# A hybrid decoder block on eight cores: list-scheduled engine queues, attention beside the gate matmuls, and an MLP in token blocks with all its weights resident

## Chip, cores, metric

One Trainium2 chip, all 8 cores, one launch. Each core computes 2048 tokens by itself; no core talks to another. The metric is device time of the slowest core in microseconds (us). Most executions agree within 0.3% (16 of the 20 runs of the kernel before lie between 920.6 and 924.6 us). In some, one die (cores 0 to 3 or 4 to 7) shows a lower granted clock and the time is longer. Such executions are called slow and stay out of all comparisons.

## The reference, cut

```python
# x: (2, 8192, 1024) float32; 8 query heads and 2 KV heads of 64; window 128; D_FF 4096
u = rms_norm(h, norm_mix)
z = u @ w_in                      # pooled groups 512 | q 512 | k 128 | v 128 | two gates of 1024
y_pool = pool_mixer(z[..., :512]) @ p_pool        # trailing means over 2, 4, 8, 16 tokens
y_attn = swa_sink_attention(q, k, v, sinks) @ p_attn   # window 128, ALiBi, one sink per head
h = h + (sigmoid(gate_pool) * y_pool + sigmoid(gate_attn) * y_attn) @ w_out
a = relu(rms_norm(h, norm_mlp) @ w_up)
h = h + (a * a) @ w_down
return rms_norm(h, norm_final)
```

## The kernel before

Bfloat16 matmuls with float32 sums. A recorder (`P.op`) notes what each operation reads and writes, derives semaphore waits, and emits each engine's instructions in the order in which the program names them. The stages follow each other over all 2048 tokens. Cut to what the argument touches:

```python
# weights, issued by GpSimd, float32 -> bf16 on the way; columns cut out of wide matrices
for g in range(4):
    dma("pool", WS[0][:, :, g*128:(g+1)*128], w_in_v[:, :, g*128:(g+1)*128], "ws0_%d" % g)
# ... and five more of this kind; x tiles are issued by SyncE:
for t in range(19):
    if t < 17:
        dma("sp", xs, src, "xs%d" % (t % 3))
        act(SQJ, xs, AF.Square, scale=1.0 / 32.0, accum=st_ss[t % 4])
    # ... power on GpSimd, scale on VectorE, transposes, then projection jobs

for i in range(19):               # attention: all 16 blocks, nothing else beside them
    if i < 16:
        att_s(i); att_exp(i)                              # scores, Exp
    if 0 <= i - 1 < 16:
        att_decay(i - 1); att_pv(i - 1); att_norm(i - 1)  # products, values, 1/sum
    if 0 <= i - 2 < 16:
        att_ot(i - 2)
# ... gates for all tokens (4 pairs of column blocks), output projection, then:
seq = [(sg, s) for sg in range(4) for s in range(4)]      # MLP: a quarter of D_FF at a time
for i in range(len(seq) + 1):
    if 1 <= i < len(seq):
        mlp_up(*seq[i])
    if i >= 1:
        mlp_down(*seq[i - 1])     # adds its part to h in SBUF: 4 evictions per output half
```

The softmax here doesn't subtract the row's maximum and nothing guards it: scores larger than these inputs give would overflow.

## Time and profile before

| | before |
|---|---|
| time, median of 20 runs beside the changed kernel | 922.3 us |
| span of the profiled run | 919.3 us |
| TensorE busy | 812.2 us (88%) |
| GpSimd busy | 219.4 us (24%) |

The prediction shows the lines behind this.

(In all lines shown, `arena` is the one SBUF tensor in which every tile of the kernel lies, so operations are told apart by engine and shape.)

### The profile page before, as it was taken

What the parts mean: (1) busy time and instruction counts of PE and PEld (TensorE: products, weight loads), DVE (VectorE), ACT (ScalarE), POOL (GpSimd) and SP (SyncE); (2) the same over time, 40 slices, a digit from 0 to 9 for tenths busy, and PEclk for the clock granted to TensorE, in tenths of its full rate; (3) what the DMA queues carried; (4) which work ended last, traced back from release to release, by engine and by line L of the source; (5) the groups of instructions that cost most, each with busy time, mean ns of one, the idle gap of its engine ahead of it and who ended that gap; (6) DMA issues with size and microseconds to landing.
All of it is one profiled execution on the core that took longest, in us unless ns stands there. A gap on an engine that the chain in (4) does not pass through costs nothing.

```text
span 919.3 us, 12450 instructions; the slowest of 8 cores (915.9 to 919.3 us)
## 1 busy us (share of the span) xinstructions
PE 812.2 (88%) x4121; PEld 377.2 (41%) x4121; DVE 359.1 (39%) x550; ACT 271.3 (30%) x439; POOL 219.4 (24%) x204
## 2 busy tenths in 40 slices
PE   1489964556999999999999999999999999999993
PEld 1344422233444444444444444444444444444441
DVE  2372166875222222256523222333223333224545
ACT  2253546543222222245531222111222111223322
POOL 3021724221232322221131111211121111113432
PEclk9999985555999999999999999999999999999997
DMA  9760009400023410199229000830009100001213
GB/s 181 157 184 2 1 8 142 80 1 1 1 23 47 52 18 1 39 222 248 43 43 163 2 1 1 123 61 1 0 1 156 28 1 1 1 1 70 91 70 137
DMA packets 37230, 55.20 MB, mean 60 GB/s; under 512 B 6960, under 2 KB 21552, under 8 KB 37168
## 3 DMA queue, kind: packets, MB, share of 16 engines
q0 software_dynamic: 28816, 27.95, 22.1%
q1 hardware_dynamic: 8352, 26.46, 8.9%
q8 instruction: 34, 0.56, 0.2%
q14 instruction: 28, 0.23, 0.1%
HBM read 73.97 MB, written 8.39 MB: 90 GB/s over the span
## 4 chain that ended last, share of the span: by engine, by line
PE 76%; DVE 11%; issue 4%; DMA 4%; ACT 3%; POOL 1%; DVEq 0%; POOLq 0%; ACTq 0%; SPq 0%
PE psum L377 74%; DVE arena L392 9%; ACT arena L388 3%; DMA arena<-w_in 3%; PE psum L381 2%; DMA arena<-x 1%; DVE arena L397 1%; POOL arena L392 1%; DVE arena L402 0%; POOL arena L412 0%; DVE arena L645 0%; DVEq L191 0%; POOLq L277 0%; ACTq L191 0%; ACT arena L407 0%
## 5 line engine op out<-in xcount | busy, mean ns | idle before, releaser
L377 PE MATMUL psum<-arena 128*128 128x512 bf16 (+2 forms) x3776 | 788.7, 374 | 67.1 <-DVE arena L392 44.4
L377 PEld LDWEIGHTS psum<-arena 128*128 128x128 bf16 x3776 | 355.3, 100 | 487.6 <-issue 95.7
L392 POOL TENSOR_TENSOR arena<-arena 128x512 bf16<-128x512 f32 (+3 forms) x167 | 191.4, 1146 | 655.1 <-ACT arena L388 339.7
L388 ACT ACTIVATE arena<-psum 128x512 f32<-128x512 f32 (+1 forms) x224 | 145.4, 658 | 439.0 <-PE psum L377 431.2
L392 DVE TENSOR_TENSOR arena<-psum,arena 128x512 f32<-128x512 f32 (+2 forms) x225 | 144.8, 654 | 164.4 <-PE psum L377 130.8
L392 DVE TENSOR_TENSOR arena<-arena 128x512 bf16<-128x512 f32 (+4 forms) x125 | 102.0, 838 | 164.0 <-ACT arena L388 161.1
L388 ACT ACTIVATE arena<-arena 128x1024 bf16<-128x1024 f32 (+1 forms) x82 | 74.3, 929 | 104.5 <-DVE arena L392 49.9
L402 DVE SCALAR_TENSOR_TENSOR arena<-arena,psum 128x512 f32<-128x512 f32 x64 | 43.8, 688 | 125.7 <-PE psum L377 122.6
L381 PE MATMUL psum<-arena 128*128 128x128 bf16 x345 | 33.2, 245 | 26.9 <-DVE arena L422 10.4
L402 DVE SCALAR_TENSOR_TENSOR arena<-arena 128x1024 f32<-128x1024 f32 (+1 forms) x20 | 29.7, 1486 | 39.7 <-POOL arena L392 23.9
L381 PEld LDWEIGHTS psum<-arena 128*128 128x128 bf16 x345 | 24.5, 110 | 41.0 <-issue 40.6
L407 ACT COPY arena<-psum 128x512 bf16<-128x512 bf16 (+3 forms) x41 | 21.9, 552 | 57.2 <-PE psum L381 36.6
L397 DVE TENSOR_SCALAR arena<-arena 128x1 f32<-128x1 f32 x66 | 19.3, 305 | 38.2 <-ACT arena L388 37.1
L402 DVE SCALAR_TENSOR_TENSOR arena<-psum,arena 128x512 f32<-128x512 f32 x32 | 22.1, 692 | 22.2 <-PE psum L377 22.2
L407 ACT CAST arena<-psum 128x512 bf16<-128x512 f32 (+1 forms) x26 | 14.6, 560 | 29.0 <-PE psum L377 28.8
L412 POOL DMA_DIRECT2D arena<-w_in x14 | 12.6, 912 | 16.5 <-DVE arena L392 15.9
L388 ACT ACTIVATE arena<-psum,arena 128x512 bf16<-128x512 f32 x16 | 11.1, 781 | 5.9 <-PE psum L377 5.9
L388 ACT ACTIVATION_READ_ACCUMULATOR arena<-arena 128x1 f32 x49 | 9.1, 186 | 0.0
L412 POOL DMA_DIRECT2D arena<-w_down x4 | 3.5, 878 | 22.5 <-PE psum L377 22.5
L645 DVE RECIPROCAL arena<-arena 128x8 f32<-128x8 f32 x16 | 3.3, 203 | 1.7
L412 POOL DMA_DIRECT2D arena<-w_up x4 | 3.8, 940 | 0.0
L412 POOL DMA_DIRECT2D arena<-p_pool x4 | 3.1, 780 | 0.0
(11 smaller groups left out, 7.5 us busy)
## 6 DMA issues: line engine op xcount, KB each, us to landing
arena<-x SPq DMA_DIRECT2D x32, 512.0 KB, 7.6
arena<-w_up POOLq DMA_DIRECT2D x4, 2048.0 KB, 18.7
arena<-w_down POOLq DMA_DIRECT2D x4, 2048.0 KB, 24.0
y<-arena SPq DMA_DIRECT2D x16, 512.0 KB, 2.6
arena<-w_in POOLq DMA_DIRECT2D x9, 512.0 KB, 11.6
arena<-w_out POOLq DMA_DIRECT2D x1, 2048.0 KB, 32.1
arena<-w_in POOLq DMA_DIRECT2D x4, 256.0 KB, 16.2
arena<-w_in POOLq DMA_DIRECT2D x1, 1024.0 KB, 30.3
```

What stands on the lines that cost most here:

```text
L377: P.op("pe", lambda e: e.matmul(out, lhsT, rhs, start=start, stop=stop), r=[lhsT, rhs], w=[out])
L381: P.op("pe", lambda e: e.transpose(out, in_, IDENT), r=[in_, IDENT], w=[out])
L388: return e.activation(out, in_, func, bias=bias, scale=scale, **kw)
L392: P.op(eng, lambda e: e.tensor_tensor(out, in0, in1, op), r=[in0, in1], w=[out])
L397: return e.tensor_scalar(out, in0, s1, None, op0)
L402: P.op(eng, lambda e: e.scalar_tensor_tensor(out, in0, scalar, in1, op0, op1), r=[in0, in1] + ([scalar] if isap(scalar) else []), w=[out])
L407: P.op("act", lambda e: e.copy(out, in_), r=[in_], w=[out])
L412: P.op(q, lambda e: e.dma_start(out=out, in_=in_), r=[in_], w=[out], dma_slot=slot)
L645: P.op("dve", lambda e: e.reciprocal(rd, den), r=[den], w=[rd])
```

## The change

Its intent: take attention, pooling and the output projection off the path by laying them between dense matmuls. A list scheduler replaces program order: every operation has a modelled cost, and each engine takes the operation that can start first among the next few in its program. Attention of block s + 1 and the output projection of block s - 1 lie in the gates of block s (512 tokens). The MLP takes one block at a time with all of `w_up` and `w_down` resident, and sums over all of D_FF in PSUM. The weights are re-laid on the host into contiguous rows. Cut to the core:

```diff
+WINDOW = {"pe": 24, "act": 24, "dve": 24, "pool": 12, "sp": 8}
+DMA_FIXED = 2.0
+DMA_RATE = 300e3
+    def schedule(self):            # ... dependency graph; then, until nothing is left:
+            for e in self.ENGINES:
+                for n in queue[e][:WINDOW[e]]:
+                    # ... t = when engine and inputs are free; keep the earliest
+            if ops[0].dma_slot is not None:
+                bus = max(bus, end) + ops[0].dma_bytes / DMA_RATE   # one bus for all DMA
+                end = bus + DMA_FIXED
-    w_in_d = din("w_in", [D, 3328])
+    wp_d = din("wp", [128, 10, 1024])   # contiguous: 2 or 4 tiles of 4 KB in one run
+    wg_d = din("wg", [8, 128, 3072])    # gate and mixer weights of one column block: 12 KB
+    wu_d = din("wu", [8, 128, 4096])    # 16 KB
+    wd_d = din("wd", [8, 128, 4096])
+    for s in range(4):
+        e = e_units(s)                             # gates of block s
+        f = f_units(s - 1) if s else []            # output projection of block s - 1
+        # ... extra: att_units of block s + 1, second norm, loads of w_up and w_down
+        run(dense, extra)
+    for s in range(4):
+        if s:
+            for fc in range(32):
+                up_unit(s, fc)
+        for ti in range(4):
+            for hh in range(2):
+                down_half(4 * s + ti, hh)          # 32 matmuls into one bank, one eviction
```

## The prediction

> **What bounds the kernel now.** I read the page from the top: busy shares, the clock row of the 40 slices, then busy time by stage (stage limits taken from the TensorE timeline), then the timeline inside the worst stage. The page:
>
> ```profile
> PE 812.2 (88%) x4121; PEld 377.2 (41%) x4121; DVE 359.1 (39%) x550; ACT 271.3 (30%) x439; POOL 219.4 (24%) x204
> ...
> PEclk9999985555999999999999999999999999999997
> ```
>
> TensorE is the only engine near its limit, and the clock row shows four slices (23 us each) at half clock. Busy time, clock and DMA in six stretches; columns are length, then busy us (instructions) of PE, PEld, DVE, ACT, POOL, then granted clock, DMA share, GB/s:
>
> ```profile
> 0.00:134.00 134.00, 91.79 (x533) 47.00 (x533) 53.56 (x70) 55.27 (x98) 39.16 (x35) 1.00 0.42 90
> 134.00:223.00 89.00, 45.84 (x389) 23.86 (x390) 64.70 (x129) 46.59 (x68) 28.70 (x25) 0.50 0.46 60
> 223.00:393.00 170.00, 170.00 (x783) 76.74 (x782) 44.53 (x65) 38.80 (x65) 47.80 (x41) 0.99 0.18 27
> 393.00:460.00 67.00, 60.88 (x356) 28.93 (x355) 39.51 (x60) 34.34 (x45) 9.36 (x17) 1.00 0.75 171
> 460.00:902.00 442.00, 439.76 (x2048) 199.51 (x2048) 147.34 (x216) 93.11 (x157) 89.91 (x84) 1.00 0.23 43
> 902.00:919.00 17.00, 3.61 (x16) 1.50 (x16) 9.09 (x13) 3.45 (x6) 4.73 (x3) 0.69 0.39 155
> ```
>
> The stretches are: first norm with projections, attention, gates, output projection, MLP, tail. Gates and MLP are solid matmul: 170.0/783 = 217.1 ns and 442/2048 = 215.8 ns for one of 512 columns. These are my unit costs. From the TensorE timeline of the first stage, eight 128-column transposes and the matmuls after them:
>
> ```profile
> 46.76 0.61 PE L381 MATMUL psum<-arena 128*128 128x128 bf16 x8 [0.29 <-DVE arena L397]
> 47.20 1.89 PE L377 MATMUL psum<-arena 128*128 128x512 bf16 x8
> ```
>
> The next instruction starts 0.44 us after the first of eight: 55 ns each. For the 65-column matmuls the trace has only half-clock groups (15 in 1.14 us, the last taking 0.21: 66 ns); 50 ns at full clock is my estimate.
>
> The program has 3472 matmuls of 512 columns (64 of them scores), 393 of 128, 256 of 65: 2048 x 0.2158 + 1424 x 0.2171 + 393 x 0.055 + 256 x 0.050 = 442.0 + 309.2 + 21.6 + 12.8 = 785.6 us. The span is 919.3, so 133.7 us are lost. By stage, length less its own work: first 134 - 84 = 50; attention 89 - 30 = 59; gates 0; output projection 67 - 59 = 8; MLP and tail 459.3 - 442 = 17. Inside attention one 128-token block takes 5 us, and TensorE waits for VectorE twice in each:
>
> ```profile
> 160.64 0.60 PE L377 MATMUL psum<-arena 128*128 128x65 bf16 x8 [1.22 <-DVE arena L392]
> 162.35 0.54 PE L377 MATMUL psum<-arena 128*128 128x65 bf16 x7 [1.10 <-DVE arena L392]
> 162.70 0.62 PE L381 MATMUL psum<-arena 128*128 128x128 bf16 x4
> 163.25 1.20 PE L377 MATMUL psum<-arena 64*128 64x512 bf16 x5
> 165.67 1.14 PE L377 MATMUL psum<-arena 128*128 128x65 bf16 x15 [1.22 <-DVE arena L392]
> ```
>
> [...] 0.50 throughout attention although these waits are only 1.1 to 1.2 us. [...] 1.00 for 442 us of dense MLP on all eight cores. [...] the 512-column product on VectorE, in attention beside GpSimd's and in the MLP window 483 to 600:
>
> ```profile
> L392 DVE TENSOR_TENSOR arena<-arena 128x512 bf16<-128x512 f32 x48 | 46.6, 1025 | 8.9 <-ACT arena L388 8.9
> ```
> ```profile
> L392 DVE TENSOR_TENSOR arena<-arena 128x512 bf16<-128x512 f32 x18 | 12.5, 692 | 46.2 <-ACT arena L388 46.2
> ```
>
> [...] So loads issued from SP and from GpSimd share the bandwidth, while the new scheduler books them one after another on a single 300 GB/s bus. [...] the share is my assumption.
>
> **The change, part by part.** Arithmetic barely moves. V comes out as 136 matmuls of 128 columns in place of 32 of 512, 8 of 128 and 17 transposes; the halo of the pooled groups shrinks to 32 of 16 columns. Now 3440 x 512, 472 x 128, 256 x 65, 32 x 16: 442.0 + 302.2 + 26.0 + 12.8 + 1.8 = 785 us. The gain has to come from the 134 us.
>
> Attention's block now lies between gate and projection matmuls. The order of the changed program has, in the gates, second scores, four or five groups of dense matmuls (4.3 to 4.8 us), then the value matmuls. What must fit there: Exp 1.02, two products of 0.69, a y product or two of 0.69, hops: 3.5 to 4.5 us. It fits, just. VectorE per 512 tokens of the middle stage: 16 x 0.69 gates + 8 x 0.69 mixes + 16 x 0.69 decays + 4 x 1.1 value norms + 11 output projection and second norm = 43 us beside 65 us of matmuls. GpSimd keeps only powers and pooling adds, so 0.69 holds. Of 59 us I leave 6 here.
>
> The start. Tiles 0 to 4 of x and the first constants are 2.9 MB, and 2.1 MB or more of weights share the bandwidth. In the output-projection stage, DMA share 1.0, 245 GB/s landed; with weights counted as the float32 read, about 325. At half of that, tile 4 lands near 3.5 + 18 = 21.7 us; square 1.25, power 0.55, scale 0.75, transposes, eviction 1.23 and hops make 5: first dense projection at 26.5 us, with 5 us of work done before. Lost: **21.5**, plus **1.7** for the cold clock.
>
> Then the order shows a fault. Because the scheduler's bus puts x tiles 6 on behind all weights, their squares stand in ScalarE's queue behind the last eviction of block 0, and the block-0 projections (20 us of matmuls) have nothing behind them. From the end of block 0 (46.5): five squares at 1.25 and two Exp pieces, then eviction of tile 8: about 56. TensorE has 1.8 us of work in these 9.3: **7.5** lost, **2** for the re-cooled clock, **2.5** for evictions queued behind late tiles in block 1.
>
> The MLP's start. The second fault in the order: three w_down pieces of 2.1 MB can load only when the output projection ends, and the last w_up piece is queued behind them. Two transfers of that kind issued together took this long in the kernel now (last column, us to landing):
>
> ```profile
> arena<-w_up POOLq DMA_DIRECT2D x4, 2048.0 KB, 18.7
> arena<-w_down POOLq DMA_DIRECT2D x4, 2048.0 KB, 24.0
> ```
>
> (2048 KB landed as bf16 is 4.2 MB read), so 8.4 MB take about 25 us and the piece lands 26 us after the projection ends. TensorE has ten groups of 1.73 and a transpose set, 17.8 us: **8** lost, **2** more for the clock.
>
> MLP: accumulating over all of K removes 96 of 128 evictions, but they lay beside matmuls, so nothing is gained but a calmer end. The tail after the last matmul is one tile: add 0.8, square 1.35, scalars and power 0.95, scale 1.4, store 3: **7.6**, in place of 17.3.
>
> Sum: 785 + 21.5 + 1.7 + 7.5 + 2 + 2.5 + 6 + 10 + 7.6 = 844 us span. The profiled time was 2.5 above the span, so **846 us**, 8% less.
>
> **The rivals.** *A: the order fits badly.* Queues are fixed in advance from modelled times. Where a tile is late, everything behind it on that engine waits, also what is ready. For: the two faults above. Against: three PSUM banks and 24-deep reordering leave slack. It would put 25 to 35 us more into the first 130: 870 to 880. *B: everything hides.* x is favoured at the DMA, the tiles come by 20 us, the waits before the MLP are covered: 785 + 15 + 3 + 8 + 2.5, some 815. Against: the static order keeps the handover gap even if data is early. *C: VectorE becomes the bound of the middle stage,* if products stay at 1025 ns: 16 x 0.33 adds 5 to 43 of 65 us. Still below, but with in-order queues it could cost 10 to 15 us: 860. [...]
>
> **Range and chances.** Uncertain are the start (plus or minus 8), the handover (0 to 12), the middle (3 to 20), the MLP's start (0 to 14). Added as independent they give about 17 to either side, and A and C lean up: 824 to 872. Faster by over 2% needs under 903, far outside A: 0.97. Within 2% 0.02, slower 0.01 [...].
>
> **What would show it.** TensorE busy share near 93%, clock row at full from the third slice on except near 50 us and one dip at the MLP's start; first run of 512-column matmuls at 24 to 29 us; a gap of 7 to 10 us near 47 to 56 us put down to VectorE; no wait of TensorE over 1.5 us in the gates; one wait of 5 to 11 us on a w_up transfer; the product group near 0.70 us; GpSimd busy below 100 us; end 7 to 9 us after the last matmul. Wrong it would be if the granted clock drops in the MLP, if middle-stage waits sum to over 20 us, or if projections are still waiting for x tiles after 70 us.

## More of the kernel before

One more view matters later and was not weighed enough: the DMA queues (queue, packets, MB landed, share of the 16 engines' time). q0 is GpSimd's queue, q1 SyncE's; weights land as bf16, half of what is read (the page's 73.97 MB read from HBM are 2 x 27.95 + 26.46 - 8.39 MB written).

```profile
q0 software_dynamic: 28816, 27.95, 21.9%
q1 hardware_dynamic: 8352, 26.46, 8.7%
```

A weight packet here is on average 27.95 MB / 28816 = 1 KB landed, 2 KB read.

## The result

| | before | after |
|---|---|---|
| time, median | 922.3 us (20 runs) | 876.4 us (10 runs) |
| ratio, 95% interval | | 0.9502 [0.9493, 0.9511] |
| TensorE busy | 88% | 91% |
| GpSimd busy | 219.4 us | 74.9 us |

A ratio is the mean time of one kernel's fast runs over that of the other's in the same rounds, so not quite the ratio of the medians. The change gains 5.0%, not 8.2%; 876 lies 4 us above the predicted range. The page of the changed kernel (40 slices of 21.9 us):

```profile
PE   0295999999999999699984999999999999999996
...
PEclk9996999999999999899996999999999999999999
DMA  8973314600212169989384212000220002200021
```

TensorE is weak only in slices 1, 2 and 4 and in two dips, slice 17 and slices 21 and 22. The DMA digit is 7 to 9 in the first three slices and where each dip begins; only slice 4 waits with little DMA under way. The four half-clock slices of attention are gone. By stage (columns as in the prediction):

```profile
0.00:45.74 45.74, 7.92 (x89) 6.63 (x90) 11.15 (x21) 8.78 (x19) 8.39 (x18) 1.00 0.95 193
45.74:66.60 20.86, 20.86 (x116) 10.40 (x116) 9.89 (x18) 7.44 (x13) 7.40 (x6) 1.00 0.67 178
66.60:79.60 13.00, 3.59 (x27) 2.45 (x27) 6.36 (x13) 9.99 (x21) 2.71 (x5) 0.65 0.35 118
79.60:147.00 67.40, 63.90 (x466) 33.94 (x467) 52.57 (x85) 39.95 (x70) 29.21 (x28) 0.97 0.29 58
147.00:344.00 197.00, 196.80 (x1161) 91.62 (x1160) 116.97 (x199) 82.83 (x122) 8.80 (x16) 1.00 0.35 80
344.00:371.00 27.00, 20.12 (x91) 8.39 (x90) 8.26 (x13) 4.69 (x7) 1.14 (x2) 0.87 0.96 200
371.00:457.70 86.70, 85.86 (x432) 39.93 (x430) 41.17 (x62) 32.42 (x51) 8.52 (x15) 1.00 0.77 161
457.70:471.00 13.30, 0.07 (x2) 0.05 (x2) 0.89 (x2) 0.60 (x1) 0.00 (x0) 0.70 0.86 141
471.00:867.70 396.70, 396.62 (x1824) 179.07 (x1824) 111.73 (x161) 76.71 (x130) 8.23 (x15) 0.99 0.11 42
867.70:875.10 7.40, 0.00 (x0) 0.00 (x0) 2.13 (x3) 1.15 (x2) 0.55 (x1) 0.83 0.17 71
```

Length less TensorE's busy time is what each stage loses, beside the prediction's term:

| stage | predicted idle | measured idle | difference |
|---|---|---|---|
| start, to the first 512-column matmul | 21.5 | 37.8 | +16.3 |
| handover from block 0 to 1 (66.6 to 79.6) | 7.5 | 9.4 | +1.9 |
| rest of block 1 and projections | 2.5 | 3.5 | +1.0 |
| gates with attention (147 to 344) | 6 | 0.2 | -5.8 |
| late gates, output projection (344 to 457.7) | 0 | 7.7 | +7.7 |
| last piece of w_up | 8 | 13.2 | +5.2 |
| MLP and tail | 7.6 | 7.5 | -0.1 |
| matmul work and slow clock (785 + 1.7 + 2 + 2) | 790.7 | 795.7 | +5.0 |

The differences sum to 31.2 of the 31.3 us between the span (875.1) and the predicted one (843.8). So attention was hidden better than predicted, and three places with a transfer pending (the start, the output projection and the last piece of w_up), with the handover and the clock, cost more. How well attention is hidden shows the TensorE timeline in the gates (start, us, operation, count): scores, values and transposes are folded into runs of 12 us without one idle entry.

```profile
163.91 0.39 PE L441 MATMUL psum<-arena 128*128 128x128 bf16 x4
164.22 11.77 PE L437 MATMUL psum<-arena 64*128 64x512 bf16 x68
175.83 0.39 PE L441 MATMUL psum<-arena 128*128 128x128 bf16 x4
176.15 11.77 PE L437 MATMUL psum<-arena 64*128 64x512 bf16 x68
```

The VectorE product, 1025 ns in attention before, is down in the same window to what the MLP showed:

```profile
L459 DVE TENSOR_TENSOR arena<-arena 128x512 bf16<-128x512 f32 x74 | 48.1, 687 | 26.3 <-ACT arena L448 24.8
```

The start is another matter. ScalarE squares each x tile as it lands; these are tiles 3, 4 and 5 (start, us; in brackets the idle time before and its cause). I had tile 4 landing at 21.7 us. Below them, the first 512-column matmuls and the first eviction of a gate, which serve as marks in the runs.

```profile
30.21 1.06 ACT L448 ACTIVATE arena<-arena 128x1024 bf16<-128x1024 f32 x1 [8.61 <-DMA arena<-x]
36.27 1.06 ACT L448 ACTIVATE arena<-arena 128x1024 bf16<-128x1024 f32 x1 [4.70 <-DMA arena<-x]
42.90 1.06 ACT L448 ACTIVATE arena<-arena 128x1024 bf16<-128x1024 f32 x1 [5.42 <-DMA arena<-x]
```
```profile
45.74 3.57 PE L437 MATMUL psum<-arena 128*128 128x512 bf16 x8 [2.23 <-DVE arena L459]
```
```profile
152.51 1.51 ACT L448 ACTIVATE arena<-psum 128x512 f32<-128x512 f32 x2 [1.20 <-PE psum L437]
```

GpSimd issues eight weight loads in the first 6 us. The DMA view of 6 to 20 us (packets, MB landed, share) says who moved:

```profile
q0 software_dynamic: 304, 1.70, 77.3%
q1 hardware_dynamic: 314, 1.10, 26.1%
```

Both queues sent nearly the same number of packets (304 and 314), but the weights' are larger: the re-layout made rows of 8 to 16 KB into one run each. As 1.70 MB landed are 3.40 MB read, SyncE's queue, which carries x, got 1.10 of 4.50 MB: 24%, where I had reckoned with half. My theory from here, from these two counts: queues that load side by side send about equally many packets, so a share goes as packet size, and the change itself starved x by enlarging the weights' packets. Rivals: simply too many bytes too early (the four gate weights); the scheduler's one-bus model of DMA, which books x behind all weights; a fixed queue order that holds loads back.

### The profile page after: what moved, and what is told of

Its sections match the earlier page's. It is cut to its first block, busy times and chain, and to the rows that moved or that the text cites. A ratio compares the mean times of both kernels' runs of the same rounds, so it can differ in the third digit from the quotient of the medians.

```text
span 875.1 us, 11943 instructions; the slowest of 8 cores (870.5 to 875.1 us)
## 1 busy us (share of the span) xinstructions
PE 795.7 (91%) x4200; PEld 372.5 (43%) x4200; DVE 361.1 (41%) x571; ACT 264.6 (30%) x434; POOL 74.9 (9%) x106
## 4 chain that ended last, share of the span: by engine, by line
PE 83%; DMA 9%; DVE 3%; issue 2%; ACT 1%; SPq 0%; POOL 0%; DVEq 0%; POOLq 0%; ACTq 0%
PE psum L437 81%; DMA arena<-x 6%; DMA arena<-wu 3%; PE psum L441 2%; DVE arena L459 1%; ACT arena L448 1%; DVE arena L471 1%; DVE arena L465 1%; SPq L482 0%; POOL arena L459 0%; DVE arena L478 0%; ACT arena L476 0%; DVEq L286 0%; POOLq L865 0%; POOL arena L482 0%
## 5 line engine op out<-in xcount | busy, mean ns | idle before, releaser
L437 PE MATMUL psum<-arena 128*128 128x512 bf16 (+3 forms) x3872 | 776.8, 362 | 37.4 <-DMA arena<-wu 13.2
L437 PEld LDWEIGHTS psum<-arena 128*128 128x128 bf16 x3872 | 349.2, 99 | 447.9 <-issue 69.9
L459 DVE TENSOR_TENSOR arena<-arena 128x512 bf16<-128x512 f32 (+4 forms) x249 | 168.8, 692 | 174.2 <-ACT arena L448 161.4
L448 ACT ACTIVATE arena<-arena 128x1024 bf16<-128x1024 f32 (+2 forms) x82 | 75.1, 928 | 290.4 <-DVE arena L459 208.2
L459 DVE TENSOR_TENSOR arena<-psum,arena 128x1024 bf16<-128x1024 bf16 (+3 forms) x97 | 75.7, 785 | 180.3 <-PE psum L437 160.2
L459 POOL TENSOR_TENSOR arena<-arena 128x1 f32<-128x1 f32 (+3 forms) x73 | 58.7, 806 | 731.8 <-DVE arena L465 634.7
L465 DVE TENSOR_SCALAR arena<-arena 128x1 f32<-128x1 f32 (+1 forms) x66 | 19.3, 306 | 72.0 <-ACT arena L448 61.9
L441 PEld LDWEIGHTS psum<-arena 128*128 128x128 bf16 x328 | 24.8, 109 | 46.7 <-issue 39.9
L471 DVE SCALAR_TENSOR_TENSOR arena<-arena 128x512 bf16<-128x512 f32 (+1 forms) x32 | 32.4, 1013 | 21.0 <-POOL arena L459 17.1
L476 ACT COPY arena<-psum 128x512 f32<-128x512 f32 (+2 forms) x36 | 19.1, 540 | 36.1 <-PE psum L437 23.4
L471 DVE SCALAR_TENSOR_TENSOR arena<-psum,arena 128x512 f32<-128x512 f32 x32 | 21.9, 688 | 15.8 <-DMA arena<-x 9.7
L476 ACT CAST arena<-psum 128x512 bf16<-128x512 f32 (+1 forms) x26 | 14.5, 562 | 21.5 <-PE psum L437 21.5
L448 ACT ACTIVATE arena<-psum,arena 128x512 bf16<-128x512 f32 x16 | 12.6, 785 | 1.1 <-PE psum L437 1.1
L482 POOL DMA_DIRECT2D arena<-wd x8 | 4.4, 547 | 21.7 <-PE psum L437 21.5
L478 DVE COPY arena<-arena 128x16 f32<-128x16 f32 x12 | 4.9, 419 | 2.3 <-ACT arena L476 2.3
## 6 DMA issues: line engine op xcount, KB each, us to landing
arena<-wg POOLq DMA_DIRECT2D x8, 768.0 KB, 22.7
```

The source lines that it names most:

```text
L437: P.op("pe", lambda e: e.matmul(out, lhsT, rhs, start=start, stop=stop), r=[lhsT, rhs], w=[out], cost=max(0.058, size(rhs) / 2400.0 + 0.0025))
L441: P.op("pe", lambda e: e.transpose(out, in_, IDENT), r=[in_, IDENT], w=[out], cost=0.058)
L448: return e.activation(out, in_, func, bias=bias, scale=scale, **kw)
L459: P.op(eng, lambda e: e.tensor_tensor(out, in0, in1, op), r=[in0, in1], w=[out], cost=vcost(eng, out, (in0, in1)) if op != ALU.pow else 0.5)
L465: return e.tensor_scalar(out, in0, s1, None, op0)
L471: P.op("dve", lambda e: e.scalar_tensor_tensor(out, in0, scalar, in1, op0, op1), r=[in0, in1] + ([scalar] if isap(scalar) else []), w=[out ...
```

## The experiments

Twelve kernels, each made from the changed kernel, all correct. Times are medians; the changed kernel's 876.4 (ratio 0.9502) is the mark.

**1. late_wg: fewer bytes early.**

```diff
+ # after scheduling: the four early gate-weight loads move in GpSimd's queue
+ move("pool", ["wg0", "wg1", "wg2", "wg3"], "after", "power of tile 16")
```

> Only the four gate-weight loads (1.6 MB each as float32) move, from the head of GpSimd's queue to behind the power of tile 16; every other queue keeps its order. Theory (the x tiles are slow because 11.6 MB of weights are queued beside them and take most of the bandwidth): tile 5 lands near 32 us in place of 42.9, first dense projection at 35 to 38 us in place of 45.7, the rest shifted by as much, 864 to 869 us. Rival (x tiles are slow by themselves, or the start hangs on the order of the queues): tile 5 lands after 40 us, 874 to 878 us.

870.2 us, ratio 0.9438 [0.9414, 0.9463]. Tile 5 was squared at 33.5 us in place of 42.9 and the first gate eviction came at 144.0 in place of 152.5: 8.5 us gained at the start, of which a new wait of 4.9 us at 393 us for an x tile took part back. The first 512-column matmul came at 42.2, not at the expected 35 to 38. Tiles 1 to 3 were as late as before (15.0, 20.4, 30.2), and in 6 to 20 us the share of x did not move, though 6.3 MB fewer were queued:

```profile
q0 software_dynamic: 299, 1.66, 77.1%
q1 hardware_dynamic: 296, 1.06, 24.9%
```

1.06 of 1.06 + 2 x 1.66 is 24% again. Bytes are part of the lateness, not the whole, and in this window, in which both queues had work, the amount queued did not set the share.

**2. small_packets: the same bytes in smaller runs.** Each row of 1024 floats gets 16 floats of padding in DRAM, so no contiguous run exceeds 4 KB.

```diff
- wu_d = din("wu", [8, 128, 4096])
+ wu_d = din("wu", [8, 128, 4, 1040])      # likewise wp, wg, wd, wo
- dma("pool", WU[i], wu_d[i].rearrange("p (c n) -> p c n", c=8), "wu%d" % i)
+ dma("pool", WUF[i], wu_d[i][:, :, 0:1024], "wu%d" % i)
```

> Same order everywhere; only the weights' rows in DRAM are padded so that no run is longer than 1024 float32 (4 KB read, 2 KB landed, as an x row's 4 KB). Theory ([...] a weight packet of 12 to 16 KB read beats an x packet of 4 KB): x gets about half, tile 5 lands at 25 to 29 us, first dense projection at 28 to 33 us, the wait for x near 344 to 371 us shrinks from 8 to under 3 us, 848 to 862 us; the wait for the last w_up piece stays at 11 to 15 us. Rival (the share follows the amount queued, not the packet): tile 5 after 40 us, 873 to 878 us.

857.0 us, ratio 0.9297 [0.9284, 0.9311]: 19 us for no change in order or bytes. Tiles 3, 4 and 5:

```profile
19.65 1.06 ACT L449 ACTIVATE arena<-arena 128x1024 bf16<-128x1024 f32 x1 [5.24 <-DMA arena<-x]
22.66 1.06 ACT L449 ACTIVATE arena<-arena 128x1024 bf16<-128x1024 f32 x1 [1.16 <-DMA arena<-x]
26.09 1.06 ACT L449 ACTIVATE arena<-arena 128x1024 bf16<-128x1024 f32 x1 [2.23 <-DMA arena<-x]
```

Tile 4 now comes at 22.7 us, near the 21.7 that I had worked out from half the bandwidth. The marks:

```profile
33.04 7.13 PE L438 MATMUL psum<-arena 128*128 128x512 bf16 x56
```
```profile
137.97 1.51 ACT L449 ACTIVATE arena<-psum 128x512 f32<-128x512 f32 x2 [1.20 <-PE psum L438]
```

In 6 to 20 us:

```profile
q1 hardware_dynamic: 673, 2.18, 53.6%
q0 software_dynamic: 553, 1.10, 49.0%
```

2.18 of 2.18 + 2 x 1.10 MB read is 50%. In the output projection VectorE's wait of 9.7 us for x became one of 1.2, with another of 3.2 at 377 us, and TensorE's idle entries between 340 and 380 us are four of 0.7 to 1.2. New waits came up: 5.8 us for projection weights, 1.9 for the pooling weights.

**3. tiny_packets: the dose.** The same with runs of 512 floats, 2 KB.

```diff
- wu_d = din("wu", [8, 128, 4, 1040])
+ wu_d = din("wu", [8, 128, 8, 528])       # likewise the others
```

> As small packets, but with the weights' rows broken at 2 KB of float32 in place of 4 KB, half of x's 4 KB. Theory ([...] the share of the bandwidth goes as the packet's size: x had about 3 tenths beside 12 to 16 KB and half beside 4 KB): x now gets two thirds, tile 4 is squared at 18 to 20 us and tile 5 at 20 to 23 (36.3 and 42.9 in the changed kernel, 22.7 and 26.1 with 4 KB), and the projection weights come later instead: the wait for them, 5.8 us with 4 KB, grows to 8 or more. 855 to 863. Rival (only the very long runs hurt, under 4 KB nothing changes): tile 5 at 25 to 27, 856 to 858.

863.3 us, ratio 0.9361 [0.9346, 0.9377]. In 6 to 20 us:

```profile
q1 hardware_dynamic: 843, 2.80, 61.4%
q0 software_dynamic: 754, 0.77, 43.5%
```

2.80 of 2.80 + 2 x 0.77 is 65%. So x had 24, 50 and 65% of the read bytes beside runs of 8 to 16, 4 and 2 KB, with packet counts equal within a quarter each time (314 to 304, 673 to 553, 843 to 754), and 310 to 321 GB/s in sum: here the share went as packet size. (These are the slowest cores of the runs; core 0 shows 25, 47 and 59%.) The time came just outside the expected range. The expected squares did not hold as dates: tile 3 was squared at 16.4 us, but 4 and 5 only at 27.4 and 28.6, behind other work of ScalarE, because TensorE stood 11.6 us for projection weights. What x gains, the weights lose: of the three sizes the middle one is the best.

The kernel before fits where its packets were of about 4 KB: in 407 to 439 us, in its output projection, its q0 sent 1373 packets (2.78 MB landed) and q1 1372. It does not fit below 2 KB: in 6 to 20 us its q0 sent 3997 packets (1.04 MB landed, so 0.5 KB read each) against 1504 of q1 (1.50 MB), so there the counts were far from equal. How the engines choose between the queues no view shows. The 3997 also speak against a rival that no run tests, that GpSimd's queue cannot deliver short packets fast enough: 553 and 754 are far below that.

**4. pitch_only: a control.** Padding moves rows in DRAM too. Here the padding stands at the end of each long row, and runs stay unbroken.

```diff
- wu_d = din("wu", [8, 128, 4096])
+ wu_d = din("wu", [8, 128, 4160])         # read [:, 0:4096]; likewise the others
```

> A control for the padding. The weights' rows in DRAM are padded by as much as in the small-packet kernel, but at the end of each row of 12 to 40 KB, so runs stay unbroken (same packet count as the changed kernel, 4176 on GpSimd's queue) and only the distance between rows changes. Theory (packet size sets the share): nothing changes, tile 5 squared at 41 to 44 us, 874 to 878. Rival (the distance between rows was what hurt, an address effect): tile 5 below 32, 856 to 866.

The fast runs took 877.6 and 878.6 us, ratio 0.9519 [0.9501, 0.9537] (two slow ones, 1026.1 and 1015.6 with one die at 0.813 to 0.842 and the other at 0.978 to 0.980, make the median useless); tile 5 at 43.7. This added distance between rows does nothing.

**5. small_early: which stage gains.** Runs of 4 KB for projection and gate weights alone.

```diff
- wp_d = din("wp", [128, 10, 1024])
+ wp_d = din("wp", [128, 10, 1040])
- wg_d = din("wg", [8, 128, 3072])
+ wg_d = din("wg", [8, 128, 3, 1040])      # wu, wd, wo as in the changed kernel
```

> Only the projection and gate weights, loaded before 150 us, have their runs broken at 4 KB; w_up, w_down and the output weights keep their long runs. It splits the 19 us of the small-packet kernel by stage. Theory: the start gives what it gave there (tile 5 at 25 to 27 us in place of 42.9, first gate eviction at 137 to 140 in place of 152.5), the 8.5 us lost to the late x tile between the gates and the output projection stay (7 to 10), the wait for w_up stays near 13: 861 to 865. Rival (a later start only moves the wait, the output projection then meets the same DMA queue earlier and loses more): 866 to 872.

862.6 us, ratio 0.9349 [0.9335, 0.9362]. First gate eviction at 138.0 (small_packets 138.0, changed kernel 152.5). TensorE's wait behind the late x tile is still there, 5.2 us at 348, and w_up's, 13.2. So about 14 of the 19 us come from the start, 5 from the output projection.

**6. hx_first: is the late x tile a matter of order?** In the changed kernel the reload of x for tile 9 stands behind the store of tile 8 in SyncE's queue, and VectorE then waits for it:

```profile
361.29 1.29 DVE L471 SCALAR_TENSOR_TENSOR arena<-psum,arena 128x512 f32<-128x512 f32 x2 [9.68 <-DMA arena<-x]
```

```diff
+ move("sp", ["x reload, tile 9"],  "before", "store of tile 8")
+ move("sp", ["x reload, tile 13"], "before", "store of tile 12")
```

> Only two entries of SyncE's queue change: the reload of x for tile 9 stands ahead of the store of tile 8, and that for tile 13 ahead of the store of tile 12. Theory (a fixed order held back a load that was ready 10 us earlier): the 8.5 us that TensorE loses between 344 and 371 us fall under 3, VectorE's longest wait for x in the output projection falls from 9.7 us under 4, and the time comes to 866 to 870. Rival (the load is slow only because w_up's large packets take the DMA engines): the load still takes 20 us, TensorE still loses 6 or more, 873 to 877.

876.6 us, ratio 0.9499 [0.9486, 0.9512]: nothing. My theory fell. SyncE's issues in this run:

```profile
339.80 0.33 SPq L499 DMA_DIRECT2D arena<-x  x1
340.37 0.33 SPq L499 DMA_DIRECT2D hres<-arena  x1
361.82 0.33 SPq L499 DMA_DIRECT2D arena<-x  x1
```

The load went out at 339.8, where it had gone at 340.5, so the store of tile 8 had not held it. The store of tile 7 had: the load reuses its buffer, and that store, issued at 325.8, took 13.9 us to land (one issued at 309.9, with no weights under way, took 2.8). Ahead of the store of tile 8 the load then took 14.0 us in place of 20.7, and VectorE waited 2.0 us for it; but that store took 21.3 in place of 12.5, and held the next reload until 361.8 (352.7 before). This one took 12.6 us, and VectorE waited for it:

```profile
374.49 0.69 DVE L488 SCALAR_TENSOR_TENSOR arena<-psum,arena 128x512 f32<-128x512 f32 x1 [8.40 <-DMA arena<-x]
```

The rival holds, in the time if not in its 20 us for the load: what SyncE's queue moves is slow beside w_up's packets, loads and stores alike. In the changed kernel it moved 2.08 MB between 344 and 371 us, and GpSimd's landed 3.29 (in 465 packets, so 14 KB read each): 2.08 of 2.08 + 2 x 3.29 is 24%, the share of the start. Run 2, which leaves the order alone, cut this wait to 1.2 us.

**7. wu7_early: the last piece of w_up first.** It stands behind three w_down pieces in GpSimd's queue. (My expectation counts 2.1 MB pieces as 4.2; three of them are 6.3 MB read.) In the changed kernel TensorE waits for it once:

```profile
470.98 29.29 PE L437 MATMUL psum<-arena 128*128 128x512 bf16 x122 [13.23 <-DMA arena<-wu]
```

```diff
+ move("pool", ["wu7"], "after", "power of tile 15, second norm")
+ move("pool", ["wd3", "wd4", "wd6"], "after", "wu7")
```

> Only GpSimd's queue changes: the last w_up piece stands ahead of the last three w_down pieces instead of behind them. Theory (the piece is late because 4.2 MB to 8.4 MB of w_down, counted as the float32 read, go first): it is issued at the same time, about 446 us, because its place in memory comes free only then, has the DMA engines to itself, takes 13 to 16 us, and TensorE waits 2 to 5 us in place of 13.2; the w_down pieces still come in time (their first use is 35 us later); 865 to 869. Rival (the bandwidth of the stage is the limit and one wait replaces another): a wait of 5 us or more for a w_down piece appears, 872 to 877.

873.2 us, ratio 0.9478 [0.9456, 0.9499]. The w_up wait is gone, and w_down's came:

```profile
472.04 1.89 PE L454 MATMUL psum<-arena 128*128 128x512 bf16 x8 [3.60 <-DMA arena<-wd]
479.33 20.90 PE L454 MATMUL psum<-arena 128*128 128x512 bf16 x86 [5.41 <-DMA arena<-wd]
```

The rival holds, 9.0 for 13.2 us. My premise that w_down is needed 35 us later was wrong: at 458 us only the last eighth of the first block's up-projection was left, so the down matmuls follow at once. In the changed kernel four pieces, 8.4 MB read, took from 438.8 to 470.8 us: 262 GB/s, where the prediction put 8.4 MB at 25 us.

**8. two_bus: the scheduler's DMA model.** One bus per issuing queue, each at half rate. Only the computed order changes.

```diff
-DMA_RATE = 300e3
+DMA_RATE = 150e3
-        bus = 0.0
+        bus = {"sp": 0.0, "pool": 0.0}
-                bus = max(bus, end) + ops[0].dma_bytes / DMA_RATE
+                bus[e] = max(bus[e], end) + ops[0].dma_bytes / DMA_RATE
```

> Only the scheduler's idea of the DMA changes: one bus of 150 GB/s for SP's loads and one for GpSimd's, in place of one of 300 for both in order of issue. Theory (the gap between blocks 0 and 1 is made by the order alone): the gap from 66.6 to 79.6 us falls from 11 us without work to under 3, the first dense projection stays at 44 to 48 us, 863 to 870 us. Rival (the tiles of block 1 are not there in time anyway): the gap stays above 8 us, 873 to 878 us.

869.6 us, ratio 0.943 [0.9416, 0.9444]. The handover gap is gone: no wait of TensorE between 43 and 100 us exceeds 2.6. The first gate eviction came at 143.8, 8.7 us earlier. The late x tiles now cost more: VectorE waited 6.0 us at 344 and 11.9 at 406.

**9. program_order: what list scheduling is worth.**

```diff
-WINDOW = {"pe": 24, "act": 24, "dve": 24, "pool": 12, "sp": 8}
+WINDOW = {"pe": 1, "act": 1, "dve": 1, "pool": 1, "sp": 1}
```

> All reordering windows set to 1, so every queue runs in program order; layout, interleaving by hand and weights as in the changed kernel. Theory (the list scheduling as such is worth a lot, its faults are those of its DMA model): block 0 then pays the norm chain of one tile, some 5 us, per projection group, 905 to 935 us. Rival (the reordering costs as much as it gives): 860 to 880 us.

985.5 us, ratio 1.0678 [1.0658, 1.0697]: slower than the kernel before, and a miss in size. TensorE waits for the first norm's scale on VectorE alone cost (total, times, longest):

```profile
PE psum L441 <- DVE arena L465: 94.9, 17, 25.2
```

There is one for each of the 17 tiles of the first norm: the program's text names each tile's norm chain just ahead of projections that do not need it. The new structure in this program order is a loss; the reordering is worth 109 us to it.

**10. small_moves: do the causes add up?** Runs 2, 6 and 7 in one.

> The small packets with both queue moves of the other two runs. If the three causes add up: small packets alone gave 857.0, of which the x reloads were already mended by the packets (so the first move gives 0 to 2 here), and the last w_up piece still cost 14.7 us (so the second gives 10 to 12): 844 to 849. Rival (the causes overlap, a wait moves on to the next): 850 to 857.

854.6 us, ratio 0.9266 [0.9253, 0.9278]: the rival's range. Both moves together gave 2.4 us over run 2, no more than run 7 alone (3.2), and run 7 trades its wait again (7.8 us for w_down).

**11. small_bus: runs 2, 7 and 8 in one.**

> Small packets, the scheduler's DMA model with one bus for each issuing queue, and the last w_up piece ahead of the three w_down pieces. Alone, the bus model took out the handover gap of 11 to 12 us after block 0 but the x tiles were as late as before. If small packets bring the tiles on time and the order now expects them so, the gap should be gone too: first gate eviction at 124 to 132 us (138.0 with small packets alone), wait for the last w_up piece under 5, 832 to 842. Rival (with tiles late at the old places, the gap moves instead of going): first gate eviction at 135 or later, 844 to 850.

840.2 us, ratio 0.9107 [0.9094, 0.9119], as the theory said: first gate eviction at 128.4. Only the wait for the MLP's weights was missed, 6.0 us for w_down in place of under 5 for w_up. The time is 17 us below small packets alone, and 14 below run 10, which has the same move of w_up but the old model: once x comes on time, an order that expects it so gains about 14 us.

**12. small_best: run 11 with two more moves.**

```diff
+ move("pool", ["wg0", "wg1", "wg2", "wg3"], "after", "power of tile 16")
+ move("pool", ["wd4", "wd6"], "after", "wu7")      # wd3 now ahead of wu7
```

> The kernel of 840 us (small packets, a bus for each issuing queue, last w_up piece early) with two more moves in GpSimd's queue: the four early gate-weight loads behind the power of tile 16, and the first of the three late w_down pieces ahead of the last w_up piece. If the wait for projection weights at 20 us is bandwidth lost to gate weights, it falls from 6.2 to under 3 and the first gate eviction comes 2 to 5 us earlier; the wait of 6.0 us for w_down falls under 3 with 0 to 3 on w_up: 831 to 837. Rival (waits trade places): 838 to 843.

835.8 us, ratio 0.9063 [0.905, 0.9077], the best kernel. TensorE and its clock:

```profile
PE   1798899999999999988999999999999999999996
...
PEclk9999999999999999999999999999999999999999
```

The reasons held by half. No wait for w_down or w_up above 0.2 us is left. But the wait for projection weights stayed (5.7 us, 6.2 before) and the first gate eviction came later, at 131.7; so gate weights were not what held the projection weights. What sets that wait is open.

## Why the prediction was wrong

Its direction and mechanism held; the sum came out 31 us short in the span, in these terms.

- **The failed step** is "The start": "At half of that, tile 4 lands near" 21.7 us. The half was a declared assumption. The share was 24% early on, tile 4 was squared at 36.3, and the first 512-column matmul came at 45.7 and not 26.5, with 16.3 us more lost before it. Shown by runs 2 to 5: with packets of equal size (4 KB) x got 50% and tile 4 comes at 22.7. What I had left out was in the diff and in the queue table of before: the re-layout turns packets of 2 KB read, on average, into runs of up to 16 KB (packets of 11 KB read on average in 6 to 20 us, 14 KB in 344 to 371). The agreement of run 2 is partly luck: 22.0 us are lost before its first 512-column matmul, for 21.5 predicted, but 5.8 of them are a wait for projection weights, which the prediction's start does not have, and that matmul still comes at 33.0. (And 3.5 + 18 is 21.5, not 21.7.) I had taken it that queues which load at the same time move equal bytes; these runs show packet counts equal within a quarter instead.
- **A loss not on the list**, 7.7 us between 344 and 457.7 us. The prediction gave the output projection no loss. It is the same cause a second time: x is reloaded beside w_up's loads, at 24% again. Runs 2, 5 and 6 tell it from a matter of order.
- **The MLP's start** was named with its piece and its cause, and mis-sized: 13.2 us for 8. Run 7 shows that bandwidth, and not only the order, is the limit: the wait moves to w_down.
- **The handover gap** was named at its place and mis-sized a little, 9.4 for 7.5. That the one-bus model makes it is shown by run 8, whose model alone removes it.
- **The middle**, 6 us predicted, cost 0.2. The claim that 3.5 to 4.5 us of attention fit between four or five dense groups was right, and so was 0.69 for the product (0.687), with GpSimd at 74.9 us. Before, it took 1.025 in attention, where GpSimd had products of its own; that those slowed it was my reading, and no run tests it alone. Rival C (VectorE as bound) is out: VectorE was busy 117 of 197 us.
- **Work and clock** came to 795.7 for 790.7. Two stretches at 0.65 (66.6 to 79.6 us) and 0.87 (344 to 371) of the clock carry some of it; I did not split the 5 us further. The predicted 1.7 agrees with the trace of the kernel before: its first eight 512-column matmuls, at 40.2 us, took 3.57 us, the eight at 47.2 took 1.89. The view of the granted clock reads 1.00 there, so that the clock is the cause is my reading; at 79.6 us of the changed kernel eight took the same 3.57 at a granted clock of 0.50. Each 2 was an estimate of mine: 3.57 less 1.89 is again 1.7 at 79.6 us, and after the wait for w_up the clock was 0.50 from 471 to 476 us, in which 13 matmuls took 5.0 us.
- **Right**: the tail (7.4 for 7.6), the MLP at 0.99 of the clock (0.99 to 1.00 on all eight cores of that execution, 471 to 867.7 us), and the chance of 0.97 on faster by over 2%.
- **A reading that was too short.** The prediction sets attention's half clock beside waits of 1.1 to 1.2 us alone. Its trace has a wait of 4.8 us just before, to 134.3 us, and one of 4.4 to 143.0; the clock was 1.00 to 133 us and 0.50 from 134. From 145 us to the end of attention no wait exceeds 1.32 us. So the short waits went with a clock that stayed at half; that they alone bring it there is not shown. It changed no term of the sum.

Rival A came nearest in size (870 to 880) but for another reason: the order's own gap cost 9.4 us, near the 7.5 predicted, while the transfers that it relied on were late. Its own form, queues fixed from modelled times, is nevertheless worth 14 us once the transfers are mended (run 11 against run 10).

## What to carry to other kernels

Here x got 24, 50 and 65% of the bytes read beside weight runs of 8 to 16, 4 and 2 KB, with packet counts equal within a quarter (0.5 KB packets of the kernel before did not fit, 3997 to 1504): before a re-layout makes one stream's runs longer, compare them with those of the stream that the first matmul needs. A list scheduler is as good as its model of DMA; give each issuing queue its own share there (here 6.8 us alone, run 8, and 14 with small packets, run 11 against 10). When a wait is taken away, look for what is needed next from the same transfers, as it may only change its name (13.2 us for w_up became 9.0 for w_down in run 7).
